# The scaling and modulation of the first norm on ScalarE

## The chip, the cores and the metric

The kernel runs on one core of a Trainium2 chip. A core has engines that run side by side, each from its own queue in order: TensorE (PE, matrix products), VectorE (DVE), ScalarE (ACT), GpSimd (POOL), and SyncE (SP), from which nearly all DMA transfers are issued. Engines wait for each other by semaphores. The metric is the device time of one execution in microseconds (us); smaller is better.

## The reference, cut to what matters

A backbone of two layers works on 512 latent tokens and 256 context tokens of 1024 features. Each layer norms its input, mixes tokens, and adds a gated feed-forward part. All shifts, scales and gates come from a conditioning vector (c for the latent tokens, c_ctx for the context):

```python
sh1, sc1, g1, sh2, sc2, g2 = adaln(c[:, None, :], mod_w[layer], mod_b[layer])   # silu(c) @ mod_w + mod_b
h = modulate(x, norm1_g[layer], sh1, sc1)          # x * rsqrt(mean(x*x) + eps) * g * (1 + sc1) + sh1
hc = modulate(ctx, norm1_g[layer], csh1, csc1)
y = gmlp_hyena_mixer(h, hyena_filter_freqs(n, ...), ...)      # layer 0
x = x + g1 * y
x = x + g2 * swiglu(modulate(x, norm2_g[layer], sh2, sc2), ffn_w_gu[layer], ffn_w_down[layer])
```

`hyena_filter_freqs` evaluates a small network at every position (it depends on weights alone), weights its result with a decay, divides by the sum of absolute values and takes a Fourier transform. Layer 0 uses the filters in a long convolution beside a gMLP; layer 1 is attention. The change concerns only `modulate` in the first norm of layer 0.

## The kernel before, in words

All products are in float32, each done as three matmuls of a high and a low part (hi*hi, lo*hi, hi*lo: L144, L146, L148, and in one helper of the gMLP all three by L815). Features lie on the 128 partitions, tokens in columns.

The program's opening stage does four things side by side. `filter_taps` and `filter_dft` make the Fourier transforms of the Hyena filters in eight rounds: a round computes six tiles of taps (matmuls, decay by DVE L572, absolute value by ACT L575, high part by ACT L588, low part by GpSimd L589, sums on DVE L577 and GpSimd L582), normalises them (L584 to L604), and multiplies them with the Fourier matrices (L144 to L148, and L626 for the skip weights). The results are copied out by ACT (L628, tile god) and DVE (L632 to L636) into a tile G and stored to DRAM by SP (L639). G has two buffers, so every third tile needs the store of the first to have landed:

```python
gl = self.t(fp, [P, 2, 2, 2, P], F32, "G", 2)
...
nc.sync.dma_start(self.G[o][cc * 2 + i][:, b0:b0 + 512], gl[:, i].rearrange("p g b c -> p (g b c)"))
```

`adaln` computes the modulation: loads of mod_w in pieces of 512 KB into a tile raw with three buffers (L330), then narrow matmuls (L332). The same raw buffers are used for the gMLP's spatial weights (freed by the transposes L839) and by the loader of all later weights (L163, with casts L166 and L167).

The first norm, with the two functions that the change touches, is laid over rounds 0 to 2 (`norm_in`, two token tiles of 128 each) and 4 to 7 (`norm_in_mod`, two feature tiles each). `norm_in` loads a token tile x, squares and sums it on ACT (L408), gets the reciprocal root on DVE and GpSimd (L362, L363), scales the tile in place (L410, per token), transposes it on PE (L414) and copies it to hT (xT in the code), half by ACT and half by DVE (L416). `norm_in_mod` applies scale and shift per feature, the 512 latent columns by DVE (L430), the 256 context columns by ACT (L432), into a tile whi, and splits it into a high part (ACT L439) and a low part (DVE L440).

The last round's products overlap the beginning of the gMLP, whose matmuls (L815, tiles pp and pc) start as soon as their weights are cast. From there to the end PE works nearly without a stop.

The order of the instructions on each engine is not the order of the code: the whole program is put in order by a simulator of the engines, with its own costs for each instruction and with priorities set in places (`tc.high_priority(offset=...)`). A different engine for a few instructions can thus reorder others on all the queues.

Of the kernel before, what the change touches and what calls it, by code (L numbers as in the profile page):

```python
# [11 lines left out]
AF = mybir.ActivationFunctionType  # L12
ALU = mybir.AluOpType
# [100 lines left out]
class Builder:  # L114
# [284 lines left out]
    def norm_in(self, xp, toks):  # L399

        nc, A = self.nc, self.A
        junk = self.big[0][0].rearrange("p a t -> p (a t)")[:, 0:D]
        for i in toks:
            x = self.t(xp, [P, D], F32, "x0", 3)
            src = A["x"][0, i * P:(i + 1) * P, :] if i < 4 else A["ctx"][0, (i - 4) * P:(i - 3) * P, :]
            nc.sync.dma_start(x, src)
            ss = self.few[:, 9 + i:10 + i]
            nc.scalar.activation(junk, x, AF.Square, accum_out=ss)  # L408
            self.rstd(ss, D, EPS)
            nc.vector.tensor_scalar(x, x, ss, None, op0=ALU.mult)  # L410
            for f0, eng in ((0, nc.scalar.copy), (4, nc.vector.tensor_copy)):
                ps = self.psA()
                for j in range(4):
                    nc.tensor.transpose(ps[:, j * P:(j + 1) * P], x[:, (f0 + j) * P:(f0 + j + 1) * P], self.eye)  # L414
                for j in range(0, 4, 2):
                    eng(self.xT[(f0 + j) // 2][:, :, i * P:(i + 1) * P], ps[:, j * P:(j + 2) * P].rearrange("p (a b) -> p a b", b=P))  # L416

    def norm_in_mod(self, fs):
        nc = self.nc
        if not fs.start:  # L420
            self.hT = []
            self.ab0 = self.modcols(0, 1)
        a, bb = self.ab0
        hs = []
        for f in range(fs.start, fs.stop):
            xT = self.xT[f // 2][:, f % 2, :]
            h = self.t(self.wp, [P, T], F32, "whi", self.wbufs[1])
            for c, sl in ((0, slice(0, NL)), (1, slice(NL, T))):
                if c == 0:
                    nc.vector.tensor_scalar(h[:, sl], xT[:, sl], a[:, f, c:c + 1], bb[:, f, c:c + 1], op0=ALU.mult, op1=ALU.add)  # L430
                else:
                    nc.scalar.activation(h[:, sl], xT[:, sl], AF.Identity, scale=a[:, f, c:c + 1], bias=bb[:, f, c:c + 1])  # L432
            hs.append(h)

        if fs.start:
            self.big.append([self.t(self.hp0, [P, 2, T], F32R, "hT", 8) for _ in "hl"])
        for f, h in zip(range(fs.start, fs.stop), hs):
            hi, lo = (x[:, f % 2, :] for x in self.big[f // 2])
            nc.scalar.copy(hi, h)  # L439
            nc.vector.tensor_sub(lo, h, hi.bitcast(F32))  # L440
            self.hT.append((hi, lo))
            self.dump("hT01", h, lambda d: d[f * P:(f + 1) * P, :])
# [928 lines left out]
```

## Time and profile before

| | |
|---|---|
| median of 3 runs | 2080.86 us (2079.05 to 2084.27) |
| the profiled execution's own time | 2078.97 us |
| its span in the trace | 2076.9 us |
| mean granted clock of PE, as a share of full | 0.978 |
| PE busy | 1957.0 us (94%) |
| DVE busy | 1165.5 us (56%) |
| ACT busy | 746.0 us (36%) |
| POOL busy | 406.8 us (20%) |

Read the busy shares with care: they are averages over stages with different limits. The edited instructions all lie in the first 104 us. A share of 36% for ACT over the whole program says nothing on how full it is there, so the rows below go by stretches. PE stands for TensorE's matmuls, PEld for its weight loads, SPq for the queue of SyncE.

### The profile page before, as it was taken

How to read it: one execution, taken by the hardware profiler on the slowest of the kernel's cores; microseconds unless marked ns; L12 is line 12 of the kernel's file. 1: busy time of each engine (PE TensorE's matmuls, PEld its weight loads, DVE VectorE, ACT ScalarE, POOL GpSimd, SP SyncE). 2: the span in 40 equal slices, each digit the busy share in tenths (PEclk: the TensorE clock that was granted, in tenths of full speed). 3: DMA queues.
4: the chain of work that ended last, by engine and by line, in shares of the span. 5: the costliest groups of instructions: out<-in, count | busy, mean ns of one | idle time of the engine just before them, and what ended most of it. 6: DMA issues, size and time to landing. Idle time of an engine off the chain costs nothing.

```text
span 2076.9 us, 28285 instructions
## 1 busy us (share of the span) xinstructions
PE 1957.0 (94%) x10995; PEld 1672.0 (81%) x10995; DVE 1165.5 (56%) x1986; ACT 746.0 (36%) x1353; POOL 406.8 (20%) x351
## 2 busy tenths in 40 slices
PE   4889999999999999689999999998989989999997
PEld 2567778899999788479989998886769978888886
DVE  5886173477787842475454444315688554444447
ACT  4654122232333321453333333214467542222222
POOL 3464000011222201233334310102150020000001
PEclk9999999999999999889999999999999999999998
DMA  7764354522222452345544545423220023333331
GB/s 257 221 215 144 104 161 163 202 79 78 71 95 85 137 183 74 91 129 164 155 145 146 159 131 188 133 80 119 62 72 1 21 82 102 88 95 105 88 110 62
DMA packets 220942, 249.04 MB, mean 120 GB/s; under 512 B 9785, under 2 KB 180394, under 8 KB 220554
## 3 DMA queue, kind: packets, MB, share of 16 engines
q1 hardware_dynamic: 220336, 241.19, 36.8%
q0 software_dynamic: 288, 5.90, 0.7%
q8 instruction: 86, 1.41, 0.3%
q14 instruction: 46, 0.38, 0.1%
q10 hardware_dynamic: 186, 0.17, 0.0%
HBM read 217.49 MB, written 29.72 MB: 119 GB/s over the span
## 4 chain that ended last, share of the span: by engine, by line
PE 87%; DMA 4%; DVE 4%; issue 2%; ACT 1%; POOL 1%; SPq 0%; DVEq 0%; POOLq 0%; ACTq 0%
PE pp L815 17%; PE pp L144 10%; PE pp L1081 9%; PE pp L146 9%; PE pp L148 9%; PE pc L1081 7%; PE pc L815 6%; PE pc L1168 5%; PE pa L332 2%; DMA raw<-in_mod_w 1%; PE pc L144 1%; PE pc L146 1%; PE pc L148 1%; PE pa L148 1%; PE pa L146 1%
## 5 line engine op out<-in xcount | busy, mean ns | idle before, releaser
L166 ACT CAST whi<-raw 128x1024 fp32r<-128x1024 f32 x164 | 171.6, 1052 | 558.9 <-PE pp L146 168.8
L167 DVE TENSOR_TENSOR wlo<-raw,whi 128x1024 fp32r<-128x1024 f32 x164 | 209.5, 1282 | 271.0 <-ACT whi L166 267.6
L908 POOL TENSOR_TENSOR xr<-xr,nh 128x512 f32<-128x512 f32 x35 | 49.1, 1430 | 797.5 <-DVE nh L907 793.2
L144 PE MATMUL pp<-hTh,whi 128*128 128x512 f32 (+1 forms) x384 | 141.3, 375 | 1.0 <-ACT hTh L393 1.0
L146 PE MATMUL pp<-hTl,whi 128*128 128x512 f32 (+1 forms) x384 | 141.2, 374 | 0.0
L148 PE MATMUL pp<-hTh,wlo 128*128 128x512 f32 (+1 forms) x384 | 139.4, 374 | 0.0
L146 PE MATMUL pp<-hT,whi 128*128 128x512 f32 (+1 forms) x512 | 136.6, 341 | 0.0
L144 PE MATMUL pp<-hT,whi 128*128 128x512 f32 (+1 forms) x512 | 135.7, 341 | 0.7 <-ACT whi L166 0.7
L148 PE MATMUL pp<-hT,wlo 128*128 128x512 f32 (+1 forms) x512 | 134.5, 340 | 0.0
L1172 DVE TENSOR_TENSOR fy<-pc,fy 128x512 f32<-128x512 f32 x72 | 48.0, 687 | 86.5 <-PE pc L1168 86.2
L1081 PE MATMUL pc<-Bh,whi 128*128 128x384 f32 x264 | 90.4, 342 | 6.3 <-ACT Bh L972 6.2
L1081 PE MATMUL pc<-Bl,whi 128*128 128x384 f32 x264 | 89.5, 340 | 2.0 <-DVE Bl L973 2.0
L144 PEld LDWEIGHTS pp<-hT,whi 128*128 128x128 f32 x512 | 79.5, 189 | 12.9 <-issue 1.2
L1081 PE MATMUL pc<-Bh,wlo 128*128 128x384 f32 x264 | 89.4, 339 | 0.0
L146 PEld LDWEIGHTS pp<-hT,whi 128*128 128x128 f32 x512 | 80.2, 189 | 10.9
L148 PEld LDWEIGHTS pp<-hT,wlo 128*128 128x128 f32 x512 | 79.7, 188 | 11.4 <-issue 1.2
L764 POOL TENSOR_TENSOR T<-T,T 128x512 f32<-128x512 f32 (+1 forms) x32 | 34.5, 1090 | 266.3 <-DVE T L763 265.2
L815 PE MATMUL pp<-whi,hT 128*128 128x512 f32 x256 | 82.3, 405 | 3.9 <-DVE G L636 2.3
L144 PEld LDWEIGHTS pp<-hTh,whi 128*128 128x128 f32 x384 | 72.3, 191 | 13.6 <-ACT hTh L393 1.2
L148 PEld LDWEIGHTS pp<-hTh,wlo 128*128 128x128 f32 x384 | 72.3, 191 | 12.6
L146 PEld LDWEIGHTS pp<-hTl,whi 128*128 128x128 f32 x384 | 72.3, 191 | 12.4
L589 POOL TENSOR_TENSOR hfsl<-hf,hfsh 128x512 fp32r<-128x512 f32 x48 | 72.0, 1518 | 48.4 <-ACT hfsh L588 25.6
(454 smaller groups left out, 5455.2 us busy)
## 6 DMA issues: line engine op xcount, KB each, us to landing
raw<-in_ffn_w_gu SPq DMA_DIRECT2D x88, 512.0 KB
raw<-in_mod_w SPq DMA_DIRECT2D x56, 512.0 KB
raw<-in_ffn_w_down SPq DMA_DIRECT2D x44, 512.0 KB
raw<-in_even_w_in SPq DMA_DIRECT2D x40, 512.0 KB
mod<-in_mod_w SPq DMA_DIRECT2D x40, 512.0 KB
G<-G SPq DMA_DIRECT2D x48, 256.0 KB
Gc<-G SPq DMA_DIRECT2D x16, 768.0 KB
raw<-act SPq DMA_DIRECT2D x32, 384.0 KB
```

The source lines that it names most:

```text
L144: mm(o, lh, rh, start=start, stop=False)
L146: mm(o, lh, rl, start=False, stop=False)
L148: mm(o, ll, rh, start=False, stop=stop)
L166: self.nc.scalar.copy(hi, raw)
L167: self.nc.vector.tensor_sub(lo, raw, hi.bitcast(F32))
L332: nc.tensor.matmul(ps[32 * j:32 * j + 32, hs], self.sc[:, k, :], raw[:, j, :], start=k == 0, stop=k == KT - 1, tile_position=(0, 32 * j))
L589: nc.gpsimd.tensor_sub(hl, hf, hh.bitcast(F32))
L815: self.nc.tensor.matmul(ps, x[:, ts], y[:, a, :], start=k + a == 0 and i == 0, stop=k + a == wk - 1 and i == 2)
L908: (eng or nc.gpsimd).tensor_add(x[:, cs], x[:, cs], tmp)
L1081: mm(ps, x[:, k, :], y[:, k, :], start=first and k == 0 and i == 0, stop=last and k == 3 and i == 2, skip_group_check=not first)
L1168: nc.tensor.matmul(ps, x[:, ts], y[:, 0, cs], start=i == 0 and j == 0, stop=i == 1 and j == 2)
L1172: nc.vector.tensor_add(ys[q][:, cs], ps, ys[q][:, cs])
```

## The change

In `norm_in` the scaling of each token tile (L410) is an ACT instruction, a copy with a scale per partition. In `norm_in_mod` the latent columns (L430) are modulated by ACT, as the context columns were before.

```diff
--- before.py
+++ after.py
@@ -407,7 +407,7 @@
             ss = self.few[:, 9 + i:10 + i]
             nc.scalar.activation(junk, x, AF.Square, accum_out=ss)
             self.rstd(ss, D, EPS)
-            nc.vector.tensor_scalar(x, x, ss, None, op0=ALU.mult)
+            nc.scalar.activation(x, x, AF.Copy, scale=ss)
             for f0, eng in ((0, nc.scalar.copy), (4, nc.vector.tensor_copy)):
                 ps = self.psA()
                 for j in range(4):
@@ -426,10 +426,7 @@
             xT = self.xT[f // 2][:, f % 2, :]
             h = self.t(self.wp, [P, T], F32, "whi", self.wbufs[1])
             for c, sl in ((0, slice(0, NL)), (1, slice(NL, T))):
-                if c == 0:
-                    nc.vector.tensor_scalar(h[:, sl], xT[:, sl], a[:, f, c:c + 1], bb[:, f, c:c + 1], op0=ALU.mult, op1=ALU.add)
-                else:
-                    nc.scalar.activation(h[:, sl], xT[:, sl], AF.Identity, scale=a[:, f, c:c + 1], bias=bb[:, f, c:c + 1])
+                nc.scalar.activation(h[:, sl], xT[:, sl], AF.Identity, scale=a[:, f, c:c + 1], bias=bb[:, f, c:c + 1])
             hs.append(h)
 
         if fs.start:
```

The six and eight instructions go to ACT's queue, and the simulated order of all the queues changes with them: on PE in the rows up to about 930 of 9828, on the others in the same stage. Behind that the order is the same. From L432 on, a line of the kernel before has a number that is 3 lower in the changed kernel (L626 is L623, L639 is L636, L815 is L812).

PE at the end of the filter stage, before (pp_2251 and pp_2290 are results of the last round's Fourier products, nrow the last sums, raw_2390 the gMLP's spatial weights, whi and wlo weights of the gMLP's input projection):

```order
L148 MATMUL pp_2309<-hfsh_2062,kf_118 128x256
L584 MATMUL pc_2015<-ab_2092,ones_119 32x256
L599 MATMUL pc_2126<-eye_85,nrow_2118 128x64 x2
L839 MATMUL pc_2394<-eye_85,raw_2390 128x128 x4
L839 MATMUL pc_2401<-eye_85,raw_2390 128x128 x4
L815 MATMUL pc_2424<-whi_2441,hT_215 128x512
L815 MATMUL pc_2424<-whi_2441,hT_216 128x512
L815 MATMUL pc_2424<-wlo_2442,hT_215 128x512
L815 MATMUL pc_2424<-whi_2441,hT_215 128x512
```

and the same place after:

```order
L148 MATMUL pp_2309<-hfsh_2062,kf_118 128x256
L596 MATMUL pc_2126<-eye_85,nrow_2118 128x64 x2
L623 MATMUL pp_2251<-snsh_2122,sel_29_121 128x256
L623 MATMUL pp_2290<-snsh_2122,sel_29_121 128x256
L623 MATMUL pp_2251<-snsl_2123,sel_29_121 128x256
L144 MATMUL pp_2251<-hfsh_2045,kf_118 128x256
L146 MATMUL pp_2251<-hfsl_2046,kf_118 128x256
L148 MATMUL pp_2251<-hfsh_2045,kf_118 128x256
L144 MATMUL pp_2251<-hfsh_2062,kf_118 128x256
```

The transposes of the spatial weights (L839, after it L836) and the first L815 stood ahead of the rest of the Fourier products; now they follow it (from row 728 on).

SP at the same place (G_23 to G_25 are the results in DRAM; raw_2709 and raw_2715 are the next two pieces of mod_w), before:

```order
L639 DMA G_23_114<-G_2211 128x512
L330 DMA raw_2709<-in_mod_w 128x4x256
L330 DMA raw_2715<-in_mod_w 128x4x256
L639 DMA G_24_115<-G_2250 128x512
L639 DMA G_25_116<-G_2250 128x512
L639 DMA G_24_115<-G_2289 128x512
L639 DMA G_25_116<-G_2289 128x512
L163 DMA raw_2721<-in_even_w_in 128x2x512
L639 DMA G_24_115<-G_2328 128x512
```

and after:

```order
L636 DMA G_23_114<-G_2211 128x512
L330 DMA raw_2709<-in_mod_w 128x4x256
L636 DMA G_24_115<-G_2250 128x512
L636 DMA G_25_116<-G_2250 128x512
L636 DMA G_24_115<-G_2289 128x512
L636 DMA G_25_116<-G_2289 128x512
L330 DMA raw_2715<-in_mod_w 128x4x256
L636 DMA G_24_115<-G_2328 128x512
L636 DMA G_25_116<-G_2328 128x512
```

The load of raw_2715 went from ahead of the last round's first four stores to behind them. The load of raw_2709 still stands ahead of them.

ACT in the middle of the stage (whi_1502, whi_1505 and whi_1746 are modulated features, A the scale from the conditioning, w3h and hfsh the high parts of filter weights and taps), before:

```order
L556 CAST w3h_1269<-w_351_1266 128x256
L416 COPY hT_211<-pp_893 128x2x128
L416 COPY hT_212<-pp_893 128x2x128
L559 ACTIVATE w3h_1269<-w3h_1269,few_95 128x256
L575 ACTIVATE ah_812<-hf_809 128x512
L559 ACTIVATE w3l_1270<-w3l_1270,few_95 128x256
L416 COPY hT_211<-pp_913 128x2x128
L416 COPY hT_212<-pp_913 128x2x128
L432 ACTIVATE whi_1502<-hT_211,modT_6_97,A_419_1500 128x256
```

and after:

```order
L154 CAST snsh_602<-snorm_600 64x256
L572 ACTIVATE ah_779<-hf_776 128x512
L585 CAST hfsh_782<-hf_776 128x512
L585 CAST hfsh_799<-hf_792 128x512
L429 ACTIVATE whi_1502<-hT_211,modT_6_97,A_419_1500 128x512
L429 ACTIVATE whi_1505<-hT_211,modT_6_97,A_419_1500 128x512
L429 ACTIVATE whi_1746<-hT_212,modT_6_97,A_419_1500 128x512
L585 CAST hfsh_816<-hf_809 128x512
L572 ACTIVATE ah_795<-hf_792 128x512
```

Three modulations of the latent columns now stand ahead of the cast of hfsh_816 and the absolute value of hf_792.

## Rows read from the trace of the kernel before

**Rows 1.** Busy time by stretch: PE, PEld, DVE, ACT, POOL, then PE's clock, DMA, GB/s.

```profile
34.00:58.00 24.00, 16.92 (x115) 9.26 (x116) 20.64 (x39) 18.91 (x42) 19.13 (x20) 0.86 0.92 297
...
76.00:104.00 28.00, 22.13 (x134) 14.99 (x133) 25.74 (x45) 21.04 (x41) 12.92 (x10) 0.88 0.56 174
...
140.00:193.00 53.00, 52.15 (x318) 40.52 (x317) 41.88 (x96) 29.14 (x61) 35.31 (x33) 1.00 0.51 170
```

**Rows 2.** Waits of PE, 36 to 210 us: total us, times, longest.

```profile
PE pa L332 <- DMA raw<-in_mod_w: 8.1, 8, 2.6
PE pp L414 <- DVE x L410: 5.4, 2, 5.0
...
PE pp L414 <- DVE hf L572: 3.1, 4, 1.9
```

**Rows 3.** Chain of waits from 192 to 221 us: start, us, what.

```profile
194.34 1.02 PE pc L839 x8
195.37 2.77 PE pc L815 x12
...
198.56 0.89 PE pc L815 x3
...
200.77 0.38 ACT god L628
...
203.58 0.34 DVE G L636
...
204.21 5.05 DMA G<-G
...
210.90 9.29 PE pp L815 x29
```

**Rows 4.** Timeline of SP's queue, 203 to 204.5 us: start, us, instruction.

```profile
203.22 0.38 SPq L330 DMA_DIRECT2D raw<-in_mod_w  x1
203.70 0.93 SPq L639 DMA_DIRECT2D G<-G  x2
```

**Rows 5.** Timeline of PE, 203 to 217 us (in brackets the wait).

```profile
207.96 0.64 PE L332 MATMUL pa<-raw,sc 128*32 128x256 f32 x8 [2.56 <-DMA raw<-in_mod_w]
...
210.90 1.19 PE L815 MATMUL pp<-whi,hT 128*128 128x512 f32 x2 [2.30 <-DVE G L636]
...
216.13 0.63 PE L815 MATMUL pp<-whi,hT 128*128 128x512 f32 x2
```

**Rows 6.** Chain of waits from 0 to 260 us.

```profile
227.21 5.44 PE pp L815 x24
```

**Rows 7.** Stretches again, columns as in Rows 1.

```profile
103.80:106.80 3.00, 2.84 (x14) 2.14 (x14) 3.00 (x8) 2.71 (x7) 2.46 (x2) 1.00 0.63 212
...
211.00:216.00 5.00, 5.00 (x12) 3.94 (x13) 0.95 (x2) 0.00 (x0) 0.00 (x0) 0.50 0.99 297
```

**Rows 8.** Groups by line and shape, 30 to 110 us: busy, mean ns, idle before.

```profile
L410 DVE TENSOR_SCALAR x<-x,few 128x1024 f32<-128x1024 f32 x6 | 6.9, 1144 | 0.7 <-POOL few L363 0.7
...
L439 ACT CAST hT<-whi 128x768 fp32r<-128x768 f32 x8 | 6.5, 830 | 0.5 <-DVE whi L430 0.5
...
L408 ACT ACTIVATE hT<-x 128x1024 fp32r<-128x1024 f32 x6 | 6.3, 1048 | 0.0
...
L430 DVE TENSOR_SCALAR whi<-hT,A,modT 128x512 f32<-128x512 f32 x8 | 6.0, 764 | 0.0
...
L432 ACT ACTIVATE whi<-hT,modT,A 128x256 f32<-128x256 f32 x8 | 4.5, 600 | 0.5 <-DVE hT L440 0.5
```

**Rows 9.** Timelines of DVE and POOL, 36 to 56 us.

```profile
40.64 1.28 POOL L589 TENSOR_TENSOR hfsl<-hf,hfsh 128x512 fp32r<-128x512 f32 x1 [0.17 <-ACT hfsh L588]
...
40.88 1.58 DVE L410 TENSOR_SCALAR x<-x,few 128x1024 f32<-128x1024 f32 x1
...
54.55 0.74 DVE L410 TENSOR_SCALAR x<-x,few 128x1024 f32<-128x1024 f32 x1
```

**Rows 10.** Timeline of PE, 103 to 107 us.

```profile
103.78 0.50 PE L144 MATMUL pp<-w3h,fHe 128*128 128x512 f32 x1 [0.68 <-DVE hf L572]
```

## The prediction

> **What bounds the kernel now.** I read the profile from coarse to fine: the busy time by stage, then what TensorE (PE) waits for, then the chain of waits around the places where the order of the queues changes, then single instructions. Most of the span is PE back to back. Already in the second half of the filter stage PE is busy 52.15 of 53 us [rows 1], so what ScalarE (ACT) or VectorE (DVE) does there is covered. The edited instructions stand earlier, at 34 to 104 us, where no engine is full alone: DVE 20.64 and ACT 18.91 of 24 us at 34 to 58, DVE 25.74 and ACT 21.04 of 28 at 76 to 104 [rows 1]. PE's waits there are short and of three kinds: 8.1 us for the loads of mod_w, 5.4 for the scaled token tile of L410 (one of them 5.0), 3.1 before the same transposes for the filter taps of L572 [rows 2].
>
> The edits reach a second place only through the order of the queues. At the end of the filter stage the chain of waits shows the last full stop of PE: PE does the L839 transposes (1.02 us from 194.34), twelve L815 matmuls (2.77) and three more (0.89) before it ends the last Fourier products; ACT copies them out at 200.77, DVE's last of the eight evictions is at 203.58, and then a store of G takes 5.05 us, for which DVE waits, since G has two buffers and the third tile wants the first [rows 3]. On SyncE (SP) the load of raw (L330) stands ahead of these stores: it could issue only at 203.22, the stores at 203.70 [rows 4]. PE stands still meanwhile but for one L332 group, waits 2.56 and 2.30 us, starts L815 again at 210.90 and does twelve matmuls until 216.13 [rows 5]. That is 5.23 us; 24 of them take 5.44 later [rows 6], so twelve should take 2.72. The granted clock was 0.50 at 211 to 216, the 1.2 GHz level [rows 7].
>
> **The change part by part.** The sum is made against the profiled execution's own 2078.97 us, 1.89 below the median of the three timed runs (2080.86); I add the 1.89 back at the end.
>
> *Taken from DVE.* Six L410 of 1.144 us mean (6.9) and eight L430 of 0.764 (6.0) [rows 8], 12.9 us in all. The long ones ran beside a GpSimd (POOL) instruction: 1.58 us at 40.88 beside L589 from 40.64, but 0.74 at 54.55 [rows 9]. I count this at nothing: the wait of 5.0 us for the first scaled tile is set by that tile's load, square sum and root before DVE may start, and the taps that DVE would bring earlier also wait for ACT and the mod_w loads. If the cover is not there, the gain is bounded by what PE waits for DVE here, 5.4 + 3.1 = 8.5 us [rows 2].
>
> *Given to ACT.* The nearest row for a 128x1024 scaling is L408 with the same shape on ACT, 1.048 us; L410's own mean on DVE, 1.144, is the other end, and I take 1.1. For a 128x512 scaling with a bias the rows either side are L432 at 256 columns (0.600) and L439 at 768 (0.830) [rows 8]; I take 0.72. That is 6 x 1.1 + 8 x 0.72 = 12.4 us. In 34 to 58 ACT would then have 18.91 + 5 x 1.1 = 24.4 of 24 us, 0.4 too much; in 76 to 104 21.04 + 5.8 = 26.8 of 28, which fits. The first scaling also queues behind the next tile's square sum (1.05 us), which the order puts ahead of it; against the 1.58 us of a disturbed scaling on DVE [rows 9] it needs 1.1, so it ends about 0.5 late. Three modulations in one row now stand ahead of a taps' cast on ACT and all wait for the one small tile A; what is queued behind them is casts that GpSimd's L589 wants. I take **+1.0 us** for this part: 0.4 and 0.5, rounded up for the queueing. The bounds: at most the whole 12.4 us (if every wait of ACT is a dependency that stays), at least −8.5 (above).
>
> The Trainium skill's page "ScalarE: Activation LUTs", section "Rules for kernel authors", speaks against this edit: add and mul belong on VectorE, which it says is faster per element. Here a row of DVE in the clear has 0.74 us for what ACT needs about 1.05 for, so the trace agrees on the single instruction; by that rule alone the kernel would get slower, and that is the rival on the other side below.
>
> *Moved: the tail of the filter stage.* In the new order PE does the remaining Fourier products right behind L599, and the L839 transposes and L815 matmuls come after; on SP the second raw load stands behind the four stores, no longer ahead of two of them. Step by step: the products end 1.02 + 2.77 + 0.89 = 4.7 us earlier, so the copy by ACT is at about 200.77 − 4.7 = 196.1 [rows 3]; 0.4 for it and four evictions of 0.34 make G's first tile ready at about 197.9. The first raw load still precedes the store on SP and waits for the transposes, which now end at about 197.6; the store goes at 198.1 where it went at 203.70 [rows 4], so 5.6 us earlier. It lands as long after its issue as before (5.5 us, of which 5.05 are the transfer), at 203.7; the third tile's evictions take the same 1.6 us from there, and L815 starts at 205.3 in place of 210.90: **−5.6 us**. Up to 204.5 PE has work of its own: the L839 transposes end at 197.6, fifteen L815 take 3.66 us [rows 3], and for the context's products and the first L332 group I take 3.2 of the 4.6 us that lie before between the copy at 200.77 and the start of the 2.56 us wait at 205.4 [rows 3, 5], since PE was not full there. So the wait before L815 shrinks from 2.30 to about 0.8 us. A wait of 0.68 us at 103.78 [rows 10] was followed by a granted clock of 1.00 over 103.8 to 106.8 [rows 7], so I expect the full 2.4 GHz after it: **−2.5 us** (5.23 − 2.72). The L332 group of the second raw load, 0.64 us at 207.96 [rows 5], stood in the idle time and now runs where PE is full: **+0.6**. Next late after that would be the weights that follow this load in the raw buffers; moved by some 5 us they keep a margin of about 4 us before PE wants them, by my estimate from their present landing. This part: −7.5. Its bounds: nothing gained, if the store stays late (+0.6), and −8.3, if the wait of 0.8 us goes too.
>
> Sum: 2078.97 + 1.0 − 7.5 = 2072.5; with 1.89 added 2074.4 against the median. From 250 us on the order is the same on every engine, so I let later stages carry the shift unchanged.
>
> **The rivals.**
> *DVE's relief shows too.* For it: DVE was the fullest engine beside PE in both stretches [rows 1], and a shared resource lengthens it. Against: the waits of PE for mod_w are as large. Half of the bound, −4.3 in place of +1.0, gives 2074.4 − 5.3 = 2069. The Trainium skill's page "SBUF — State Buffer", section "SBUF: two separate sides", states that DVE and GpSimd share a port pair that one of them holds alone for a whole instruction; 1.58 against 0.74 us for L410 agrees. By it GpSimd gets quicker as well.
> *The tail is not gained.* The raw load ahead of the store may issue late, since it waits for transposes that now stand behind the Fourier products, or the transfer may be slowed by others; then L815 starts where it did. 2078.97 + 1.0 + 0.6 + 1.89 = 2082.5.
> *ACT becomes the bound of the early part, the other side.* One mechanism: ACT's waits there are dependencies that stay, and all 12.4 us (rounded to 13 with its instruction gaps) land on the chain taps, square sum, scale, transposes. For it: ACT overfull in 34 to 58. Against: 5.1 and 7 us idle in the two stretches, and PE's slack of waits. It gives 2074.4 − 1.0 + 13 = 2086; it makes the kernel slower than before as soon as the early loss is above 7.5 us.
> *The change does not do what it says:* excluded, since the order lists all fourteen instructions on ACT.
>
> **How the numbers follow.** Forecast 0.52 (2074.4, its own range 2070 to 2078), relief too 0.14 (2069), tail not gained 0.20 (2082.5), ACT bound 0.14 (2086). A measurement of this kernel can tell some 0.3% from no change, 6.2 us: faster is below 2074.6, slower above 2087.1. The forecast stands on that border, so half of it counts as faster: 0.26 + 0.13 + 0.02 = 0.41; slower 0.08, the upper part of the last case; the same 0.51. The range of 8 in 10 leaves out half of the ACT case and a small part of the relief case: 2066 to 2085.
>
> **What would show it.** In the changed profile: L815 after the last eviction of the third G tile starts about 6 us earlier relative to L599, with a wait under 1.2 us and a clock of 1.00 behind it (right), or again after more than 2 us at 0.50 (wrong). Relative to the first matmul, L599 itself comes 1 us later (right), 4 earlier (relief) or 7 and more later (ACT bound). ACT at 34 to 58 is busy nearly throughout, DVE at about 14.5 us of 24. The prediction is wrong if the difference arises after 260 us, where the order is unchanged.

## The result and the profile after

The changed kernel takes 2068.61 us (median of five runs, 2068.01 to 2073.07) against 2083.09 of the kernel before, measured beside it (2079.05 to 2084.27). The ratio is 0.994, with a 95% interval of 0.9927 to 0.9953. The time is inside the range, but at the number of the rival in which VectorE's relief shows as well (2069), not at the forecast's 2074.4: about twice the gain that was forecast. The profiled execution took 2068.01 us with a span of 2065.9, which is 11.0 less than before.

First the busy time of the engines in the stretches of [rows 1], columns as there:

```profile
34.00:58.00 24.00, 16.20 (x108) 8.94 (x108) 12.66 (x31) 22.31 (x44) 16.62 (x18) 0.84 0.94 312
58.00:76.00 18.00, 18.00 (x123) 12.52 (x123) 11.64 (x31) 10.51 (x22) 7.99 (x10) 0.92 0.84 263
76.00:104.00 28.00, 23.50 (x154) 16.55 (x152) 22.73 (x44) 26.86 (x53) 14.62 (x13) 1.00 0.62 193
104.00:140.00 36.00, 30.49 (x207) 21.84 (x207) 30.39 (x65) 22.31 (x44) 18.53 (x18) 1.00 0.72 228
140.00:193.00 53.00, 52.67 (x328) 42.24 (x325) 41.04 (x100) 29.55 (x63) 32.42 (x30) 1.00 0.47 160
```

ACT is about as full as was worked out (22.3 of 24 us for 24.4, 26.9 of 28 for 26.8), and it costs little: at 76 to 104 us PE is busier than before (23.50 for 22.13), and its clock is 1.00 where it was 0.88. The two stretches that [rows 1] leave out were, before:

```profile
58.00:76.00 18.00, 18.00 (x125) 13.20 (x125) 12.04 (x34) 8.77 (x19) 8.47 (x10) 1.00 0.93 288
...
104.00:140.00 36.00, 31.47 (x203) 23.31 (x203) 29.49 (x60) 20.79 (x43) 24.71 (x18) 0.95 0.71 225
```

The groups by line and shape, to be held against [rows 8], and the two GpSimd groups of both kernels (changed kernel first, then before):

```profile
L586 POOL TENSOR_TENSOR hfsl<-hf,hfsh 128x512 fp32r<-128x512 f32 x21 | 27.8, 1337 | 30.6 <-DVE hf L569 21.3 <-ACT hfsh L585 9.4
...
L410 ACT ACTIVATE x<-x,few 128x1024 f32<-128x1024 f32 x6 | 6.9, 1147 | 0.2 <-POOL few L363 0.2
...
L429 ACT ACTIVATE whi<-hT,modT,A 128x512 f32<-128x512 f32 x8 | 6.4, 821 | 0.3 <-DVE A L357 0.3
...
L363 POOL TENSOR_TENSOR few<-few 128x1 f32<-128x1 f32 x6 | 3.3, 555 | 6.1 <-DVE few L362 6.1
```

```profile
L589 POOL TENSOR_TENSOR hfsl<-hf,hfsh 128x512 fp32r<-128x512 f32 x20 | 33.3, 1680 | 35.1 <-DVE hf L572 20.5 <-ACT hfsh L588 14.6
...
L363 POOL TENSOR_TENSOR few<-few 128x1 f32<-128x1 f32 x6 | 4.1, 689 | 0.0
```

The added instructions cost ACT 6.9 + 6.4 = 13.3 us (12.4 were reckoned). GpSimd's low parts fell from 1.68 to 1.34 us each, though nothing was changed on GpSimd.

How far the kernel is at the end of the filter stage is told by the last transposes of the sums, L599 before and L596 after. Up to them PE has the same work to do in both orders. First the timeline of PE before, then after:

```profile
194.01 0.33 PE L599 MATMUL pc<-eye,nrow 64*128 64x64 f32 x2 [0.51 <-DVE nrow L592]
```

```profile
189.80 0.33 PE L596 MATMUL pc<-eye,nrow 64*128 64x64 f32 x2
```

So 4.2 us are gained by then. The chain of waits behind it, for [rows 3]:

```profile
189.87 0.26 PE pc L596 x2
...
192.65 0.87 PE pc L836 x8
193.53 3.89 PE pc L812 x17
...
199.70 0.57 PE pa L332 x8
200.27 9.52 PE pp L812 x41
```

There is nothing but PE in it: the store of G, the evictions and ACT's copy are off the chain. SP's queue shows why (before: [rows 4]); the second row of the timeline of DVE is the third tile of G, which now waits for ACT's copy and no longer for the store [rows 3]:

```profile
193.56 0.38 SPq L330 DMA_DIRECT2D raw<-in_mod_w  x1
194.03 2.43 SPq L636 DMA_DIRECT2D G<-G  x4
200.33 0.38 SPq L330 DMA_DIRECT2D raw<-in_mod_w  x1
```

```profile
194.27 0.41 DVE L633 TENSOR_TENSOR G<-god,pp 128x256 f32<-128x256 f32 x1
199.28 0.42 DVE L629 TENSOR_TENSOR G<-pp,god 128x256 f32<-128x256 f32 x1 [4.60 <-ACT god L625]
```

L812 on tile pp starts at 200.2, 10.4 us behind L596, where it was 16.9 us behind L599 [rows 5]: 6.5 us more. The low clock behind the stop is gone, as the same stretch shows, before and after:

```profile
193.00:216.00 23.00, 17.63 (x88) 12.55 (x88) 6.85 (x20) 3.52 (x9) 0.00 (x0) 0.85 0.55 167
```

```profile
193.00:216.00 23.00, 23.00 (x115) 18.65 (x114) 6.53 (x14) 4.39 (x8) 0.00 (x0) 1.00 0.59 201
```

Each matmul compared with the same one before, the shift is 13.1 us at 220 us. It then falls where the L332 group of the second raw load now takes PE's time (before it stood in the idle time, at 207.96 us [rows 5]):

```profile
237.14 0.64 PE L332 MATMUL pa<-raw,sc 128*32 128x256 f32 x8
```

Towards the end of the gMLP's projection the shift is 12.4 us (the last product of whi and hT on tile pp starts at 805.1 instead of 817.5). A small part is lost at 680 to 720 us, where PE's order differs by a few matmuls once more; that the order is the same from 250 us on is not quite right. At 1424 us the shift is 12.1, at 1541 us 10.3, although the order is unchanged there (PE's clock at 1440 to 1540 us was 0.98 before and 0.93 after); some of it comes back by 1700 us, and 11.0 reach the end.

### The profile page after: what moved, and what is told of

Same layout as the page of the kernel before. It is cut to its first block, busy times and chain, and to the rows that moved or that the text cites. A ratio compares the mean times of both kernels' runs of the same rounds, so it can differ in the third digit from the quotient of the medians.

```text
span 2065.9 us, 28285 instructions
## 1 busy us (share of the span) xinstructions
PE 1953.7 (95%) x10995; PEld 1671.7 (81%) x10995; DVE 1151.3 (56%) x1972; ACT 756.7 (37%) x1367; POOL 398.7 (19%) x351
## 4 chain that ended last, share of the span: by engine, by line
PE 87%; DVE 4%; DMA 4%; issue 2%; ACT 1%; POOL 1%; SPq 0%; DVEq 0%; POOLq 0%; ACTq 0%
PE pp L812 17%; PE pp L144 9%; PE pp L146 9%; PE pp L148 9%; PE pp L1078 9%; PE pc L1078 7%; PE pc L812 6%; PE pc L1165 5%; PE pa L332 2%; PE pc L144 1%; PE pc L146 1%; PE pc L148 1%; DMA raw<-in_mod_w 1%; PE pa L146 1%; PE pa L148 1%
## 5 line engine op out<-in xcount | busy, mean ns | idle before, releaser
L812 PE MATMUL pp<-whi,hT 128*128 128x512 f32 x256 | 80.3, 396 | 1.9 <-ACT whi L166 1.9
L146 PEld LDWEIGHTS pp<-hTl,whi 128*128 128x128 f32 x384 | 72.0, 190 | 12.4
L586 POOL TENSOR_TENSOR hfsl<-hf,hfsh 128x512 fp32r<-128x512 f32 x48 | 63.6, 1339 | 45.6 <-ACT hfsh L585 22.8
```

The costliest lines, as they stand in the source:

```text
L146: mm(o, lh, rl, start=False, stop=False)
L586: nc.gpsimd.tensor_sub(hl, hf, hh.bitcast(F32))
L812: self.nc.tensor.matmul(ps, x[:, ts], y[:, a, :], start=k + a == 0 and i == 0, stop=k + a == wk - 1 and i == 2)
```

## The experiments

The change does two things at once: it moves fourteen instructions to another engine, and it makes the scheduler order all queues anew. To part them, the order was written into the kernel. Every instruction keeps its name in both kernels, so the names of a wanted order can be chained; the edges order the issue on one engine and make nobody wait for a result:

```diff
+def _pin(tc, nc):
+    by = {i.name: i for i in nc.cur_bb.bb.instructions}
+    for run in _ORDER.values():
+        run = [x for x in run if f"I-{x}" in by]
+        for x, y in zip(run, run[1:]):
+            tc.add_manual_dep(by[f"I-{y}"], f"I-{x}", mybir.DependencyInfo(mybir.DependencyClass.NoSync, mybir.DependencyReason.DATA), reason="pinned")
...
         Builder(tc, aps, out).build()
+        _pin(tc, nc)
```

`_ORDER` holds one list of names for each engine. The fourteen instructions are not in the lists: they find their places beside them. "Early" is the order up to about 185 us, "tail" what follows.

Each ratio is to executions of the kernel before made beside the run. Their medians were 2082.6 to 2083.1 us; only beside "L430, order before" it was 2086.1. Each trace is of one execution, and not always a typical one: those of the kernel before and of the changed kernel are faster than nearly all of theirs, that of the order alone (2078.1 us, median 2073.7) and that of early order and engine are the slowest. So the ratios carry the verdicts, and a trace tells of a mechanism only where several agree.

| early order | tail order | L410 on | L430 on | ratio, 95% interval | run |
|---|---|---|---|---|---|
| before | changed | DVE | DVE | 0.9972, 0.9958 to 0.9986 | tail order |
| changed | before | ACT | ACT | 0.9971, 0.9957 to 0.9984 | early order and engine |
| before | before | ACT | ACT | 0.9981, 0.9968 to 0.9994 | engine alone |
| before | before | DVE | ACT | 0.9963, 0.9948 to 0.9978 | L430, order before |
| changed | changed | DVE | DVE | 0.9952, 0.9933 to 0.9970 | order alone |
| changed | changed | ACT | DVE | 0.9957, 0.9945 to 0.9969 | L410 alone |
| changed | changed | DVE | ACT | 0.9943, 0.9929 to 0.9957 | L430 alone |
| changed | changed | ACT | ACT | 0.9940, 0.9927 to 0.9953 | the changed kernel |

**The tail.** The kernel before, with the changed kernel's order from about 185 us on:

```diff
+_ORDER = {...}     # names of the kernel before up to 185 us, then of the changed kernel
```

> The fourteen instructions stay on VectorE and everything up to about 185 us is issued in the order of the kernel before; from there on (the last Fourier products, the transposes of the spatial weights, the first gMLP matmuls, the raw loads and the stores of G) every queue has the order of the changed kernel. Theory A (the tail's gain comes from the order of the queues alone): the whole tail part, 8.2 us by the two profiles, so a ratio of about 0.996, L815 after the third tile of G without a stop and a clock of 1.00 behind it. Theory B (the tail was gained because the ACT version reaches it in another state): under 3 us.

It measured 0.9972, 5.8 us of the 2083, with an interval of 2.9 to 8.7: theory A, if somewhat under its 8.2 us. The timelines of SP and PE of this run test the hand chain of the prediction directly, since the early part is that of before:

```profile
198.03 0.38 SPq L330 DMA_DIRECT2D raw<-in_mod_w  x1
198.51 2.90 SPq L639 DMA_DIRECT2D G<-G  x4
```

```profile
205.33 0.70 PE L815 MATMUL pp<-whi,hT 128*128 128x512 f32 x2 [0.59 <-DVE G L636]
```

The store was forecast for 198.1, L815 for 205.3 with a wait of 0.8 us. All the runs agree on this part: from the last sums' transposes to the first such product on tile pp it takes 14.2 to 16.9 us in the five traces with the tail's order of before, and 10.4 to 11.2 in the eight with the changed one.

The reverse, the changed kernel with the tail's order of before:

```diff
+_ORDER = {...}     # names of the changed kernel up to 185 us, then of the kernel before
```

> The changed kernel, but from about 185 us on every queue has the order of the kernel before. Theory A: the tail's 8.2 us are lost again, 4.2 stay: a ratio of about 0.998, with PE stopping about 5 us for the store of G and a low clock behind it. Theory B: near the changed kernel, 0.994 to 0.995.

0.9971 lies between the two ratios that were named, nearer to theory A: the tail's part is lost again (0.9940 to 0.9971, 6.5 us). The stop of about 5 us for the store that was expected is not in its trace: PE waits 2.43 us for the raw load, the first product on pp comes 14.4 us behind the transposes, and the clock at 193 to 216 us is 0.93.

Which queue does it? The kernel before with SP's order alone:

```diff
+_ORDER = {...}     # names of the kernel before; of SP from 185 us on those of the changed kernel
```

> The kernel before, but SyncE alone has the order of the changed kernel at the end of the filter stage: the second raw load goes behind the four stores of G. TensorE keeps its order, so the transposes and the first L815 stay ahead of the last Fourier products. If the raw load ahead of the store was what cost the time, the store goes out 1 us earlier and the ratio is 0.9995, at most 0.998 where the stop gets short enough for the clock to stay up. If TensorE's order is what counts, no more than 1 us is gained and the second raw load now lands later: 0.9995 to 1.001, with a stop of 4 to 6 us before L815 as before.

1.0003 (0.9994 to 1.0012): nothing. The timeline of PE shows the wait that took the place of the one for the store:

```profile
206.59 1.08 PE L332 MATMUL pa<-raw,sc 128*32 128x256 f32 x8 [3.43 <-DMA raw<-in_mod_w]
207.60 1.22 PE L815 MATMUL pp<-whi,hT 128*128 128x512 f32 x2
```

L815 starts 15.8 us behind L599 (191.8) instead of 16.9, and PE has stood still for the raw load instead. So SP's order is not enough by itself. That PE's order, with the work of the gMLP behind the Fourier products, covers both transfers is read from the traces. PE's order alone, with SP's of before, was not tried: the two orders wait for each other in a circle.

**Engine or order in the early part.** The engines of the changed kernel in the order of before:

```diff
-            nc.vector.tensor_scalar(x, x, ss, None, op0=ALU.mult)
+            nc.scalar.activation(x, x, AF.Copy, scale=ss)
...
-                if c == 0:
-                    nc.vector.tensor_scalar(h[:, sl], xT[:, sl], a[:, f, c:c + 1], bb[:, f, c:c + 1], op0=ALU.mult, op1=ALU.add)
+_ORDER = {...}     # names of the kernel before throughout
```

> The fourteen instructions run on ScalarE as in the changed kernel, but all the others stand in the order of the kernel before on every queue. Relief theory (a freer VectorE and a freer GpSimd bring the early 4.2 us): about 4 us faster than before, 0.998. Order theory (the early gain is one of order): 0 to 6 us slower than before, 1.000 to 1.003, since ScalarE carries 13.5 us more in queues that were ordered without it. Clock theory (the gain is that three waits of PE fell under 2 us and the clock stayed up): either way, and the granted clock at 80 to 120 us tells: 1.00 with a gain, 0.8 with none.

0.9981 (0.9968 to 0.9994): faster by 4 us, without any help of an order. This is the relief theory's number; ACT's added 13 us cost nothing that shows. The trace is a poor witness here: in this execution the second load of mod_w came 7 us late in the opening (PE's wait at 23.10 us is 7.05, before it is 0.31), so its last transposes are not comparable. The clock theory's mark is at neither of its values: 0.91 at 80 to 120 us, in an execution that is among the slowest of this run (2082.8 us, median 2078.6).

The order alone, with all fourteen on VectorE:

```diff
+_ORDER = {...}     # names of the changed kernel throughout
```

> The fourteen instructions stay on VectorE, and all the others stand in the order of the changed kernel on every queue. Order theory: nearly the whole gain, a ratio of 0.994 to 0.995. Relief theory: the tail's 8.2 us but not the early 4.2, a ratio of about 0.996, with L410 at 1.1 us mean on VectorE again and L599 of the last round as late as before (194 us). Clock theory: 0.996 where PE's clock falls at 80 to 120 us, 0.994 where it does not.

0.9952, in the middle between the order theory and the relief theory. L599 is at 195.2 us in the profiled execution, the slowest of the six, no earlier than before (194.0), which is the relief theory's mark; of the ratio 0.0028 is the tail, and the other 0.0020 is within the two intervals. The windows at 104 to 118 us (changed kernel, then this run) show PE a little longer busy with fewer matmuls, at a lower clock:

```profile
104.00:118.00 14.00, 11.00 (x80) 8.73 (x81) 12.65 (x25) 8.90 (x17) 5.74 (x7) 1.00 0.60 185
```

```profile
104.00:118.00 14.00, 11.70 (x68) 9.77 (x68) 13.62 (x27) 8.92 (x17) 4.23 (x4) 0.76 0.49 158
```

**Which half, and is it VectorE's load?** In the order of the changed kernel, only L410 on ACT, only L430 on ACT, and both on ACT with VectorE's load put back:

```diff
+            nc.scalar.activation(x, x, AF.Copy, scale=ss)          # L410 alone; L430 as before
```

> Only the six scalings of the token tiles (L410) are on ScalarE; the eight modulations (L430) stay on VectorE; all other instructions stand in the order of the changed kernel. If the relief of VectorE comes from the first stretch (34 to 58 us, L410 beside GpSimd's L589), most of the early gain is here: L599 of the last round near 190 us and a ratio of 0.994 to 0.995. If it comes from the second stretch (76 to 104 us, where VectorE was busy 25.7 of 28 us), L599 stays at 194 to 195 as in the kernel with the order alone, and the ratio is 0.995 to 0.996.

```diff
+                nc.scalar.activation(h[:, sl], xT[:, sl], AF.Identity, scale=a[:, f, c:c + 1], bias=bb[:, f, c:c + 1])   # L430 alone; L410 as before
```

> The other half: only the eight modulations (L430) are on ScalarE, the six scalings (L410) on VectorE, the order that of the changed kernel. Relief in the second stretch: L599 of the last round near 191 us, 0.994 to 0.995. Relief in the first: 194 to 195 us, 0.995 to 0.996. Clock theory: neither half decides, and L599 goes with the clock at 76 to 140 us alone.

```diff
             nc.scalar.activation(x, x, AF.Copy, scale=ss)
+            dj = self.big[0][1].rearrange("p a t -> p (a t)")[:, 0:D]
+            _EXTRA.add(nc.vector.tensor_scalar(dj, x, ss, None, op0=ALU.mult).ins.name)
...
             hi, lo = (x[:, f % 2, :] for x in self.big[f // 2])
+            _EXTRA.add(nc.vector.tensor_scalar(lo[:, 0:NL], self.xT[f // 2][:, f % 2, 0:NL], a[:, f, 0:1], bb[:, f, 0:1], op0=ALU.mult, op1=ALU.add).ins.name)
```

(`_EXTRA` keeps the added instructions out of the lists.) The load put back is not quite the old one: 9.5 us on VectorE where it was 12.9, and VectorE waits 1.0 us for ACT's scaled tiles.

> The changed kernel in its own order, but VectorE also does fourteen instructions of the same shapes as before (six of 128x1024, eight of 128x512) into columns that nobody reads yet; ScalarE's results are the ones used, so no consumer waits for VectorE. Theory of load (what was gained early is VectorE's time and GpSimd's undisturbed access): the gain goes back to that of the order alone, 0.995 to 0.996, with L599 of the last round at 193 to 196 us and GpSimd's L589 at 1.6 to 1.7 us mean instead of 1.34. Theory of latency (what was gained is that the scaled tiles come earlier from ScalarE): it stays at 0.994, L599 at 190.

The three measured 0.9957, 0.9943 and 0.9964 (0.9950 to 0.9978). The last sums' transposes, in the timelines of PE of these runs, in the same sequence:

```profile
196.57 0.33 PE L599 MATMUL pc<-eye,nrow 64*128 64x64 f32 x2
```

```profile
189.20 0.33 PE L596 MATMUL pc<-eye,nrow 64*128 64x64 f32 x2
```

```profile
194.33 0.33 PE L599 MATMUL pc<-eye,nrow 64*128 64x64 f32 x2
```

In one order, the transposes come early where L430 is on ACT (189.2, and 189.8 with both), and late where it is not (196.6) or where VectorE's load is put back (194.3), although ACT's results are the ones used there. These places alone do not show the cause: part of the lag is there before the modulations begin, and kernels with the same early part spread by 2.5 us (191.8 to 194.3 us in three traces). What VectorE holds up can be read more directly, from PE's waits for its taps (hf) at 76 to 140 us, before and then after:

```profile
PE pp L144 <- DVE hf L572: 2.9, 3, 2.0
PE pp L414 <- DVE hf L572: 2.1, 2, 1.9
```

```profile
PE pp L144 <- DVE hf L569: 2.5, 3, 0.9
```

| in the changed order | second round's transposes, us | last transposes, us | PE's waits for taps at 76 to 140 us |
|---|---|---|---|
| the changed kernel | 74.9 | 189.8 | 2.5 |
| L430 alone on ACT | 73.2 | 189.2 | 1.9 |
| load put back | 76.8 | 194.3 | 4.4 |
| L410 alone on ACT | 77.6 | 196.6 | 4.4 |
| order alone | 74.4 | 195.2 | 5.0 |

Over all fourteen traces these waits are 3.9 to 5.7 us in the seven in which VectorE does work of L430's size and 1.9 to 3.5 in the seven in which it does not, whatever the order. So what L430 takes from PE is VectorE's time at 76 to 140 us. The ratios say less: those of L410 and L430 alone point the same way, but their intervals overlap; that of the load put back lies 0.0024 (5 us) above the changed kernel's, and its interval just touches it. The clock theory does not hold: a clock of 0.97 at 76 to 140 us goes with 189.2 (L430 alone) and with 194.3 (load put back). The mark for GpSimd was missed: with the load back its low parts take 1.44 us, not 1.6 to 1.7, and with the order alone, L410 and L430 on VectorE, 1.51; the order has a part in their 1.34.

L430 alone was tried in the order of before as well:

```diff
+_ORDER = {...}     # L430 on ACT; names of the kernel before throughout
```

> Only L430 goes to ScalarE, and all other instructions stand in the order of the kernel before on every queue, the tail too. If the early gain is VectorE's relief at 76 to 104 us, it is here as well: L599 of the last round 3 to 5 us earlier than before, counted from the end of the first loads, the stop before L812 of tile pp as before, and a ratio of 0.998. If the early gain needs the new order, L599 stays within 1 us and the ratio is 0.9995 to 1.001.

0.9963 (0.9948 to 0.9978): the gain does not need the new order. The mark that was named failed in the one profiled execution (2080.7 us, median 2078.2): its L596 is at 196.1, with a clock of 0.76 at 104 to 118 us, though PE's waits for taps are shorter here too (3.5 us). The distance to the first product on pp was 14.2 us, not 16.9. Its executions spread from 2072 to 2083 us.

**A step further in the same direction.** The low parts of the modulated columns on GpSimd:

```diff
-            nc.vector.tensor_sub(lo, h, hi.bitcast(F32))
+            nc.gpsimd.tensor_sub(lo, h, hi.bitcast(F32))
```

> The changed kernel in its order, with the eight low parts of the modulated columns (VectorE, 1.2 us each) on GpSimd as well. If VectorE's load alone decides the stretch of 76 to 140 us, another 9.6 us less on it brings a further 1 to 4 us: 0.992 to 0.994. If GpSimd's own queue (the low parts of the taps, which TensorE needs) or the sharing between the two engines counts as much, eight instructions of about 2 us in that queue delay the taps: 0.995 to 1.000, with TensorE waiting for hfsl.

0.9953, no better than the changed kernel, and the second theory's number. Its mechanism was not seen: PE does not wait for hfsl in this trace, and its one wait for hf is 2.5 us long. The group on GpSimd costs more than on VectorE (1.21 us before, 1.09 in the changed kernel):

```profile
L437 POOL TENSOR_TENSOR hT<-whi,hT 128x768 fp32r<-128x768 f32 x8 | 16.3, 2047 | 1.3 <-ACT hT L436 1.3
```

**What the scheduler makes of either half.** Without lists, as one would write it:

```diff
+            nc.scalar.activation(x, x, AF.Copy, scale=ss)          # L410 alone, no pinned order
```

> Only L410 goes to ScalarE, and the simulated scheduler orders the queues itself. It leaves the tail as in the kernel before: the transposes and L815 ahead of the last Fourier products, the second raw load ahead of the stores. Theory (all of the gain is that of L430: VectorE's relief at 76 to 104 us, and the order of the tail that comes with it): no gain, 0.999 to 1.002. If the scalings had a share of their own: 0.997 to 0.998.

```diff
+                nc.scalar.activation(h[:, sl], xT[:, sl], AF.Identity, scale=a[:, f, c:c + 1], bias=bb[:, f, c:c + 1])   # L430 alone, no pinned order
```

> Only L430 goes to ScalarE, and the simulated scheduler orders the queues itself; the tail comes out as in the changed kernel. The same theory: the whole gain, 0.994 to 0.995, with L599 of the last round at 189 to 191 us and no stop before the first L812 of tile pp. If the scalings had a share of their own: 0.996 to 0.997.

L410 alone: 0.9972 (0.9958 to 0.9986), though the tail stays as before. So the theory that all the gain is L430's is too strong: L410, or the early order that came with it, has a share, too. L430 alone: 0.9909 (0.9891 to 0.9927), 2064.86 us, more than expected, with the last transposes at 187.0 us (189 to 191 was named). It is the best version: all its executions (2063.05 to 2066.93) are below all of the changed kernel (from 2068.01). The windows of this run:

```profile
34.00:58.00 24.00, 16.61 (x116) 9.54 (x117) 20.57 (x39) 19.19 (x42) 19.30 (x20) 0.93 0.88 289
58.00:76.00 18.00, 18.00 (x126) 13.14 (x125) 12.01 (x34) 8.78 (x19) 8.44 (x10) 1.00 0.90 288
76.00:104.00 28.00, 21.54 (x146) 14.91 (x144) 21.59 (x44) 26.20 (x51) 15.47 (x12) 0.98 0.62 201
104.00:140.00 36.00, 34.90 (x211) 26.00 (x212) 31.36 (x64) 23.79 (x47) 21.11 (x19) 0.92 0.74 243
```

Its first stretch is that of before (the order is the same there), it has the relief at 76 to 104 and the changed tail, and at 104 to 140 us PE stands still for only 1.1 us where the changed kernel has 5.5. In the changed kernel's order the same half gave 0.9943, so the rest is this order's. Why it has so few stops there was not tested.

## Why the prediction was right, and where not

The forecast was a change of −6.5 us; about twice that was measured. The tail came as worked out; the rest came from a term that the prediction had put at nothing.

*The tail: right, in mechanism and nearly in size.* −7.5 was forecast. In the two profiles the first L812 on pp comes 6.5 us nearer to L596 (5.6 were forecast with a wait of 0.8 left over, and that wait is gone as well), the clock behind it brings about 2.4 (2.5), and the L332 group of the second raw load takes its 0.64 at 237 us (0.6): some 8.3 in all. By the ratios it is less, 5.8 (2.9 to 8.7) and 6.5 us; in other executions with the tail's order of before the distance was 14.2 us, not 16.9. The chain worked out by hand holds to half a microsecond where the early part was left as it was (store 198.5, L815 205.3, wait 0.59). It needs PE's order: SP's order alone gave nothing.

*Taken from DVE: wrong.* "I count this at nothing" is the step that failed. The reason given, that the first scaled tile's wait of 5 us is set by its own load and sums, is right (5.4 us after, now behind ACT), and it speaks of L410. For L430, at 76 to 104 us, stood only that the taps also wait for ACT and the loads, though the row had VectorE busy 25.74 of 28 us [rows 1]. PE's waits were not of three kinds: the rows from which [rows 2] were taken have one more for VectorE's taps, and its longest ends at 111.85 us, behind the stretch that was looked at:

```profile
PE pp L144 <- DVE hf L572: 3.2, 4, 2.0
```

With it the bound of 8.5 us is 11.7. The early part measured −4.2 in the profile, on the mark of 4 us that the prediction gave for the relief; by the ratios 4 us with both groups on ACT in the order of before, and 8 with L430 alone, each to within some 3 us; +1.0 was forecast. This was the rival with a chance of 0.14 and a price of −4.3. That price was half of a bound that was read too low, so its fit is luck.

*How it pays.* Against expectation hardly by less standing still. From 34 us to the last transposes PE does 890 matmuls in both kernels (before, then after):

```profile
34.00:194.00 160.00, 141.16 (x890) 101.29 (x890) 130.25 (x272) 98.65 (x204) 100.55 (x87) 0.95 0.67 215
```

```profile
34.00:189.80 155.80, 137.66 (x890) 99.29 (x890) 116.99 (x259) 110.69 (x220) 90.18 (x87) 0.97 0.68 220
```

It is idle for 18.8 and 18.1 us, and busy for 3.5 us less. Its waits for taps are shorter, but it now waits for other results of VectorE. The granted clock at 76 to 104 and 104 to 140 us was 0.88 and 0.95 before and 1.00 after, and some is given back at 58 to 76 us (1.00 to 0.92). So in these two executions most of the 4.2 us is time that PE lost to the 1.2 GHz level and now does not. With the spread between executions the division is not settled.

*Given to ACT: right.* 13.3 us for 12.4, 1.15 and 0.82 each for 1.1 and 0.72. ACT was nearly full and no bound; the rival in which all its time lands on the chain is refuted by the engines alone (0.9981, faster).

*Carried to the end: nearly.* 12.4 us at 805 us became 11.0 at the end; the order on PE was not quite the same from 250 us on.

## What to carry to other kernels

Ask of each edited instruction in which stretch it stands and which engine is fullest there beside PE; one sentence of cover per line, not one for both. Where a scheduler orders the queues, a change of engine is two changes: pin the order, and measure the engine and the order each by itself; here the order alone gave 0.9952, the engines alone 0.9981, both 0.9940. Try the halves of a change alone, too: the half that relieves the full engine gave as much as both in one order (0.9943), and 0.9909 with the order that the scheduler made for it.

## What the runs showed of the hardware

A stop of about 2 us was not always followed by a low clock. The timelines of PE in the kernel before and in the changed kernel have two of nearly the same length, each ending in a first product of the taps:

```profile
111.85 0.36 PE L144 MATMUL pp<-hfsh,kf 128*128 128x256 f32 x1 [2.05 <-DVE hf L572]
```

```profile
105.62 0.36 PE L144 MATMUL pp<-hfsh,kf 128*128 128x256 f32 x1 [2.01 <-DVE rr L598]
```

The windows of three microseconds behind them, in the same sequence:

```profile
111.80:114.80 3.00, 2.95 (x22) 2.22 (x22) 3.00 (x6) 0.34 (x2) 2.12 (x2) 0.81 0.49 144
```

```profile
105.60:108.60 3.00, 2.98 (x20) 2.60 (x20) 3.00 (x7) 2.53 (x4) 0.00 (x0) 1.00 0.22 59
```

The length of the stop alone does not tell what the clock does. And executions of one kernel spread further than the three runs shown at first (2079 to 2084): the kernel before itself ran from 2078 to 2092 us beside the other runs, the engines alone from 2076 to 2085, the L430 half in the order of before from 2072 to 2083. A load of 512 KB in the opening for which PE waited 6.3 and 7.1 us in two of the traces (early order and engine, engine alone) may be one part of that; this was not tested.
